# Weights split in plain order with strided views of PSUM, and stationary columns taken 4 and 2 apart, in a two-layer encoder trunk

## Chip, core and metric

The kernel runs on one core of one Trainium2 chip. The metric is the device time of one execution in microseconds; the median of three runs of the kernel before is 1271.1 us (1270.49 to 1271.89).

## What is computed

A trunk of two layers over 256 positions of width 1024. Each layer is a half-step feed-forward part, a mixer and another half-step feed-forward part, each with a norm ahead of it and one behind it. The mixer is dilated window attention in layer 0 and two-way retention in layer 1.

```python
def rms_norm(x, g):
    y = x * lax.rsqrt(jnp.mean(x * x, axis=-1, keepdims=True) + NORM_EPS)
    return y * g

def swiglu(h, w_gate, w_up, w_down):
    return (jax.nn.silu(h @ w_gate) * (h @ w_up)) @ w_down

for i in range(DEPTH):                       # DEPTH = 2, D = 1024, D_FF = 2816
    g = norm_gains[i]
    h = swiglu(rms_norm(x, g[0]), ffn_w_gate[i, 0], ffn_w_up[i, 0], ffn_w_down[i, 0])
    x = x + 0.5 * rms_norm(h, g[1])
    hm = rms_norm(x, g[2])
    m = dilated_attention(hm, ...) if i % 2 == 0 else retention(hm, ...)
    x = x + rms_norm(m, g[3])
    h = swiglu(rms_norm(x, g[4]), ffn_w_gate[i, 1], ffn_w_up[i, 1], ffn_w_down[i, 1])
    x = x + 0.5 * rms_norm(h, g[5])
```

The order of the 2816 inner columns of a feed-forward part is free, as long as the rows of its down matrix come in the same order.

## The kernel before

All weights are read once from memory, 235 MB, in groups of 1 MB into two `raw` buffers (`Stream.dma`). A group has two pieces of 1024 numbers per partition. `Stream.split` makes each piece into a rounded high part (ScalarE, lines 131 and 137) and the rest as low part (VectorE, lines 132 and 138), in a ring of six `w` tiles, and for the first pieces of a part in spare tiles (`wx`). Every product of activations with weights is then three matmuls: high by high, low by high, high by low. With a gain (lines 137 and 138) a piece is split in two instructions of 512, without one (down and output matrices, lines 131 and 132) in one of 1024.

There are two forms of product. In the first (`piece`, `mm3`, lines 217 to 219) the activations are stationary and 512 weight columns move; the down matrices, attention's v, retention's v and gates, and the first two units of each feed-forward part are computed so. In the second (`unit_t`, lines 414 to 416) the weights are stationary, a block of 128 columns at a time, and 256 positions move; units 2 to 10 of each feed-forward part and attention's and retention's q and k are computed so. Pieces for the second form are called `still`. A part has ten units of 512 columns (gate and up in turn, `h` for a pair) and an eleventh of 256 gate and 256 up columns.

The moving operand is always read with `alternate`: one element from the first half of the columns, one from the second. In the first form the split therefore reads `raw` with `deal`, two elements apart, and writes two halves, so that the columns land in PSUM in their own order. In the second form the positions land in PSUM in alternating order, and `tiles` reads them from there two apart.

At the end of a part `down` finishes the first 128 positions (`t` = 0) of the last five rows ahead of the second; `post` takes the square sum of each half on ScalarE (line 295) and the product with the gain on VectorE (line 296), then a few Newton steps, and adds to `x` (line 302). `pre_half` transposes the new `x` on TensorE (line 259) into the next part's `xh` and `xl`. ScalarE and VectorE run their instructions in the order given; the splits of the next part's first weights stand between those of `post`. In the first two units of a part the transposes of the first `h` (`h_store`, line 449) wait for `row_end` (line 432), a row of the norm's scales.

Of the kernel before, what the change touches and what calls it, by code (L numbers as in the profile page):

```python
# [14 lines left out]
P = 128  # L15
# [11 lines left out]
def deal(z):  # L27

    return z.rearrange("p (h c a) -> p h a c", a=2, c=256)


def halves(z):
    return z.rearrange("p (h a c) -> p h a c", a=2, c=256)


def alternate(z):

    return z.rearrange("p (a c) -> p c a", a=2)


class Stream:
# [18 lines left out]
    def add_rows(self, srcs, rows, norm, still=False):  # L60

        first = len(self.pieces)
        for k0 in range(0, rows, 4):
            g = len(self.groups)
            self.groups.append(("rows", srcs, k0))
# [7 lines left out]
    def add_down(self, src, rows):  # L73

        first = len(self.pieces)
        for k0 in range(0, rows, 2):
            g = len(self.groups)
            self.groups.append(("down", src, k0))
            for j in range(2):
                self.pieces.append((g, j, None))  # L80
        return list(range(first, len(self.pieces)))

    def dma(self, halves=False, queue=None):
        if self.n_dma >= len(self.groups):
            return
        kind, src, k0 = self.groups[self.n_dma]
        nc = self.K.nc
        queue = queue or nc.sync
        raw = self.K.sb.tile([P, 2048], F32, tag="raw", bufs=self.raw_bufs, name=f"raw{self.n_dma}")
        if kind == "rows":  # L90
            r = raw.rearrange("p (k c) -> p k c", k=4)
            c = 0
            for ap in src:
                w = ap.shape[1]
                n = 2 if halves else 4
                for i in range(0, 4, n):
                    queue.dma_start(
                        r[:, i : i + n, c : c + w],
                        ap[(k0 + i) * P : (k0 + i + n) * P, :].rearrange("(k p) c -> p k c", p=P),
                    )  # L100
                c += w
        else:
            nc.sync.dma_start(
                raw.rearrange("p (k c) -> p k c", k=2),
                src[k0 * P : (k0 + 2) * P, :].rearrange("(k p) c -> p k c", p=P),
            )
        self.raw[self.n_dma] = raw
        self.n_dma += 1

    def split(self):  # L110
# [16 lines left out]

        view = (lambda z: z) if i in self.still else deal
        flat = (lambda z: z) if i in self.still else halves
        if gain is None:  # L130
            nc.scalar.activation(flat(hi), view(raw), AF.Copy)  # L131
            nc.vector.tensor_tensor(out=flat(lo), in0=view(raw), in1=flat(hi).bitcast(F32), op=ALU.subtract)  # L132
        else:
            for kk in range(2):
                s = slice(kk * 512, kk * 512 + 512)
                gc = self.K.gcol[:, gain + kk : gain + kk + 1]
                nc.scalar.activation(flat(hi[:, s]), view(raw[:, s]), AF.Copy, scale=gc)  # L137
                nc.vector.scalar_tensor_tensor(  # L138
                    out=flat(lo[:, s]), in0=view(raw[:, s]), scalar=gc, in1=flat(hi[:, s]).bitcast(F32),
                    op0=ALU.mult, op1=ALU.subtract,  # L140
                )
# [21 lines left out]
class Trunk:  # L163
# [123 lines left out]
    def post(self, t, banks, gb, name, eps=None):  # L287
# [48 lines left out]

    def plan_ffn(self, l, i):
# [8 lines left out]
        return dict(units=units, down=self.ws.add_down(wd, DFF // P), l=l, n=n)  # L346
# [18 lines left out]
    def ffn_t(self, u, pieces, name, natural, st):  # L365
# [4 lines left out]
        self.unit_t(pieces, accs)  # L370
# [29 lines left out]
    def unit_t(self, pieces, accs, quota=2):  # L400
# [3 lines left out]
        for j, pc in enumerate(pieces):  # L404
            hi, lo = self.ws.get(pc)
            for kk in range(2):
                k = 2 * j + kk
                xh, xl = (alternate(z[:, k, 0 : 2 * P]) for z in (self.xh, self.xl))
                for c in range(4):
                    b, a = divmod(c, 2)  # L410
                    out = accs[b][:, a * 256 : a * 256 + 256]
                    s = slice(kk * 512 + c * P, kk * 512 + c * P + P)

                    mm(out, hi[:, s], xh, start=k == 0 and a == 0, stop=False, skip_group_check=True)  # L414
                    mm(out, hi[:, s], xl, start=False, stop=False, skip_group_check=True)  # L415
                    mm(out, lo[:, s], xh, start=False, stop=k == NK - 1, skip_group_check=True)  # L416
# [26 lines left out]
    def h_store(self, c, t, h, w, natural):  # L443
# [4 lines left out]
        for k in range(nk):  # L448
            nc.tensor.transpose(tr[:, k * P : (k + 1) * P], h[:, k * P : (k + 1) * P], self.ident)
# [25 lines left out]
    def ffn(self, plan, nxt):  # L475
        nc, sb = self.nc, self.sb
        l, n = plan["l"], plan["n"]
        name = f"f{l}{n}"
        natural = l == 0 and n % 6 == 4
        st = {}  # L480
        for u, pieces in enumerate(plan["units"]):
# [17 lines left out]
            if u == 0:  # L499
                sg = []  # L500
                for t in range(2):
                    g = sb.tile([P, 512], F32, tag="sg", bufs=2, name=f"sg_{name}{c}{t}")
                    nc.scalar.activation(g, accs[t], AF.Silu, scale=self.rstd[:, t : t + 1])
                    sg.append(g)
            else:
                self.pend.append(lambda: self.row_end(name))
                for t in range(2):
                    h = sb.tile([P, 512], F32, tag="h", bufs=2, name=f"h_{name}{c}{t}")
                    nc.vector.tensor_tensor(out=h, in0=accs[t], in1=sg[t], op=ALU.mult)
# [139 lines left out]
    def attn(self, plan, nxt):  # L649
# [5 lines left out]
        for u, (o, kind, g, pieces) in enumerate(plan["units"]):  # L655
# [28 lines left out]
            if kind != "v":  # L684
# [14 lines left out]
                for t in range(2 if u == 0 else 0):  # L699
                    nat = sb.tile([P, 512], F32, tag="h", bufs=2, name=f"nat{u}{t}")  # L700
                    nc.scalar.activation(nat, accs[t], AF.Copy, scale=(rq if kind == "q" else self.rstd)[:, t : t + 1])
# [17 lines left out]
            else:  # L719
                if g == 0:  # L720
                    V = sb.tile([P, 6, 512], F32, tag="D", name=f"V{o}")
                    for t in range(2):
                        nc.vector.tensor_scalar(out=V[:, t, :], in0=accs[t], scalar1=self.rstd[:, t : t + 1], scalar2=None, op0=ALU.mult)
                else:

                    for t in range(2):
                        rs = self.rstd if g == 1 else ru
                        for half in range(2):
                            r = 2 * t + half if g == 1 else (2 * t + 1 + half) % 4
                            hs = slice(half * 64, half * 64 + 64)  # L730
                            if half == 0:
                                nc.vector.tensor_scalar(out=V[hs, 2 + r, :], in0=accs[t][hs, :], scalar1=rs[hs, t : t + 1], scalar2=None, op0=ALU.mult)
                            else:
                                nc.scalar.activation(V[hs, 2 + r, :], accs[t][hs, :], AF.Copy, scale=rs[hs, t : t + 1])
# [162 lines left out]
    def ret(self, plan, nxt):  # L897
# [6 lines left out]
        for u, (h, kind, pieces) in enumerate(plan["units"]):  # L904
# [16 lines left out]
            elif kind == "v":  # L921
                vv = sb.tile([P, 2, 2, 512], F32R, tag="C1", name=f"vv{h}")
                st["vh"], st["vl"] = vv[:, 0], vv[:, 1]
                for t in range(2):
                    rs = self.rstd[:, t : t + 1]
                    vh, vl = (halves(st[z][:, t, :]) for z in ("vh", "vl"))
                    nc.scalar.activation(vh, deal(accs[t]), AF.Copy, scale=rs)
                    nc.vector.scalar_tensor_tensor(out=vl, in0=deal(accs[t]), scalar=rs, in1=vh.bitcast(F32), op0=ALU.mult, op1=ALU.subtract)
# [3 lines left out]
            else:  # L932
                d = 0 if kind == "gf" else 1
                sg = []
                for t in range(2):
                    g = sb.tile([P, 512], F32, tag="sg", bufs=2, name=f"rsg{u}{t}")
                    nc.scalar.activation(g, accs[t], AF.Silu, scale=self.rstd[:, t : t + 1])
# [55 lines left out]
    def rt_gate(self, st, d, sg):  # L993
# [9 lines left out]
        for t in range(2):  # L1003
            if d == 0:
                w = st["C2"][:, 512 * t : 512 * t + 512]
                st["w", t] = w
                nc.vector.scalar_tensor_tensor(out=w, in0=st["y", d][t], scalar=mv[:, t, 0:1], in1=sg[t], op0=ALU.subtract, op1=ALU.mult)
                nc.vector.tensor_scalar(out=w, in0=w, scalar1=r[:, t : t + 1], scalar2=None, op0=ALU.mult)
            else:
                nc.vector.scalar_tensor_tensor(out=sg[t], in0=st["y", d][t], scalar=mv[:, t, 0:1], in1=sg[t], op0=ALU.subtract, op1=ALU.mult)  # L1010
# [77 lines left out]
```

## Time and profile before

| | us |
|---|---|
| median of three runs | 1271.1 |
| the profiled execution, own time | 1272.25 |
| its span, first to last instruction | 1270.5 |
| TensorE matmul busy | 1228.0 |
| weight loads busy | 1125.8 |
| VectorE busy | 941.8 |
| ScalarE busy | 789.0 |
| DMA queue of the weights, share of 16 engines | 57% |

Busy time of matmuls counts overlapping ones as one stretch, so the rate of TensorE is read from the starts of neighbouring matmuls. Weight loads overlap matmuls. The chain of waits follows the work back from the last instruction to whatever released it; where it runs through an engine other than TensorE, the time of that engine sets when TensorE may go on.

### The profile page before, as it was taken

Reading aid. Unit: us, or ns where it says so; the run is one execution under the profiler, and the core shown is the slowest. Engines: PE = TensorE matmul, PEld = TensorE weight load, DVE = VectorE, ACT = ScalarE, POOL = GpSimd, SP = SyncE. Lnnn points to the kernel's source line nnn. Section 1 sums busy time; section 2 is a strip of 40 time slices with the busy share of each in tenths; the row PEclk is TensorE's granted clock in tenths of the full one; section 3 lists DMA queues with packets and bytes.
Section 4 is the critical chain, followed back from the end, with each engine's and each line's share of the span. In section 5 each row is a group of like instructions: output and inputs, shape, how many; then the busy total and the mean of one; then the engine's idle time right before and its main releaser. Section 6 shows DMA issues by size and latency. Waiting matters only on the chain.

```text
span 1270.5 us, 21059 instructions
## 1 busy us (share of the span) xinstructions
PE 1228.0 (97%) x8532; PEld 1125.8 (89%) x8532; DVE 941.8 (74%) x1615; ACT 789.0 (62%) x1065; POOL 19.4 (2%) x17
## 2 busy tenths in 40 slices
PE   8999999999999999999989999998999999999997
PEld 7999987977998778999879999887998988899986
DVE  6776668678568868887577766688999987776665
ACT  6656665467456666876666666655766767565662
POOL 1000001000000000000000000000000000000000
PEclk9999999999999999999999999999999999999999
DMA  7756566763764355665646665645565546466552
GB/s 219 235 179 198 192 211 182 228 206 117 216 216 166 122 165 190 194 217 196 202 137 221 195 197 196 204 145 168 168 185 175 166 167 209 142 228 200 192 196 77
DMA packets 130270, 235.75 MB, mean 186 GB/s; under 512 B 25451, under 2 KB 42075, under 8 KB 130172
## 3 DMA queue, kind: packets, MB, share of 16 engines
q1 hardware_dynamic: 129372, 233.04, 57.0%
q8 instruction: 67, 1.10, 0.3%
q10 hardware_dynamic: 800, 1.36, 0.3%
q14 instruction: 31, 0.25, 0.1%
HBM read 232.21 MB, written 1.12 MB: 184 GB/s over the span
## 4 chain that ended last, share of the span: by engine, by line
PE 71%; DVE 15%; DMA 8%; ACT 5%; issue 1%; DVEq 0%; POOL 0%; ACTq 0%; SPq 0%; POOLq 0%
PE ac_f L416 9%; PE ac_f L414 9%; PE ac_f L415 9%; DVE w L138 7%; PE d_f L217 5%; PE d_f L219 5%; PE d_f L218 5%; DMA raw<-in_ffn_w_gate_dram 4%; PE rt L219 3%; PE rt L217 3%; PE rt L218 3%; PE at L414 3%; PE at L416 3%; PE at L415 3%; ACT w L137 1%
## 5 line engine op out<-in xcount | busy, mean ns | idle before, releaser
L137 ACT ACTIVATE w<-raw,gcol 128x512 fp32r<-128x512 f32 x596 | 427.6, 777 | 253.7 <-PE ac_f L416 72.6
L138 DVE SCALAR_TENSOR_TENSOR w<-raw,gcol,w 128x512 fp32r<-128x512 f32 x596 | 437.6, 781 | 134.0 <-ACT w L137 131.9
L132 DVE TENSOR_TENSOR w<-raw,w 128x1024 fp32r<-128x1024 f32 x112 | 166.9, 1492 | 97.2 <-ACT w L131 96.2
L131 ACT ACTIVATE w<-raw 128x1024 fp32r<-128x1024 f32 x112 | 174.4, 1561 | 100.3 <-DMA raw<-in_ffn_w_down_dram 38.6
L217 PE MATMUL d_f<-w,hhf 128*128 128x512 f32 x352 | 134.7, 383 | 0.0
L218 PE MATMUL d_f<-w,hhf 128*128 128x512 f32 x352 | 134.4, 382 | 0.0
L219 PE MATMUL d_f<-w,hlf 128*128 128x512 f32 x352 | 134.2, 381 | 0.0
L414 PE MATMUL at<-xh_f,w 128*128 128x256 f32 x352 | 96.9, 276 | 0.0
L415 PE MATMUL at<-xl_f,w 128*128 128x256 f32 x352 | 96.9, 275 | 0.0
L416 PE MATMUL at<-xh_f,w 128*128 128x256 f32 x352 | 96.8, 275 | 0.0
L414 PE MATMUL ac_f<-xh_in,w 128*128 128x256 f32 x288 | 79.6, 276 | 0.0
L416 PE MATMUL ac_f<-xh_in,w 128*128 128x256 f32 x288 | 79.4, 276 | 0.0
L414 PE MATMUL ac_f<-xh_f,w 128*128 128x256 f32 x288 | 79.3, 275 | 0.0
L415 PE MATMUL ac_f<-xl_at,w 128*128 128x256 f32 x288 | 79.3, 275 | 0.0
L415 PE MATMUL ac_f<-xl_f,w 128*128 128x256 f32 x288 | 79.3, 275 | 0.0
L415 PE MATMUL ac_f<-xl_rt,w 128*128 128x256 f32 x288 | 79.3, 275 | 0.0
L414 PE MATMUL ac_f<-xh_at,w 128*128 128x256 f32 x288 | 79.3, 275 | 0.0
L414 PE MATMUL ac_f<-xh_rt,w 128*128 128x256 f32 x288 | 79.3, 275 | 0.0
L416 PE MATMUL ac_f<-xh_at,w 128*128 128x256 f32 x288 | 79.2, 275 | 0.0
L416 PE MATMUL ac_f<-xh_f,w 128*128 128x256 f32 x288 | 79.2, 275 | 0.0
L415 PE MATMUL ac_f<-xl_in,w 128*128 128x256 f32 x288 | 79.2, 275 | 0.0
L416 PE MATMUL ac_f<-xh_rt,w 128*128 128x256 f32 x288 | 79.2, 275 | 0.0
(350 smaller groups left out, 2971.0 us busy)
## 6 DMA issues: line engine op xcount, KB each, us to landing
raw<-in_ffn_w_down_dram SPq DMA_DIRECT2D x44, 1024.0 KB, 4.8
raw<-in_ffn_w_up_dram SPq DMA_DIRECT2D x40, 1024.0 KB, 5.0
raw<-in_ffn_w_gate_dram SPq DMA_DIRECT2D x39, 1024.0 KB, 5.0
raw<-in_attn_w_in_dram SPq DMA_DIRECT2D x36, 1024.0 KB, 5.1
raw<-in_ret_w_in_dram SPq DMA_DIRECT2D x24, 1024.0 KB, 5.4
raw<-in_ret_w_in_dram SPq DMA_DIRECT2D x16, 512.0 KB, 4.5
raw<-in_ret_w_out_dram SPq DMA_DIRECT2D x8, 1024.0 KB, 4.7
raw<-in_ffn_w_gate_dram SPq DMA_DIRECT2D x8, 512.0 KB, 3.9
```

The costliest lines, as they stand in the source:

```text
L131: nc.scalar.activation(flat(hi), view(raw), AF.Copy)
L132: nc.vector.tensor_tensor(out=flat(lo), in0=view(raw), in1=flat(hi).bitcast(F32), op=ALU.subtract)
L137: nc.scalar.activation(flat(hi[:, s]), view(raw[:, s]), AF.Copy, scale=gc)
L138: nc.vector.scalar_tensor_tensor(out=flat(lo[:, s]), in0=view(raw[:, s]), scalar=gc, in1=flat(hi[:, s]).bitcast(F32), op0=ALU.mult, op1=AL ...
L217: mm(out, xh, wh, start=start, stop=False)
L218: mm(out, xh, wl, start=False, stop=False)
L219: mm(out, xl, wh, start=False, stop=stop)
L414: mm(out, hi[:, s], xh, start=k == 0 and a == 0, stop=False, skip_group_check=True)
L415: mm(out, hi[:, s], xl, start=False, stop=False, skip_group_check=True)
L416: mm(out, lo[:, s], xh, start=False, stop=k == NK - 1, skip_group_check=True)
```

## The change

`Stream.split` no longer deals: every piece is read and written in plain order. The moving weights are still read with `alternate`, so their columns now land in PSUM in alternating order, and whoever reads such a bank does it through `undo`, two elements apart: post-norm, gate, h, attention's first q and k and its V, retention's v, gates and the group-norm products. Square sums and group-norm statistics read a bank as before.

In `unit_t` the 128 stationary columns of a block may lie `step` apart. `STEPS` gives 4 for the first feed-forward part, 2 for the second and 1 for the other two; the eleventh unit takes at most 2. This changes the order of the inner columns, so `h_store` transposes the same columns, and the down matrix is loaded so that a partition takes `step` neighbouring rows, two of them in one load (8 KB in a row). Retention's and attention's blocks keep step 1.

The order of instructions is the same on TensorE, VectorE, ScalarE and GpSimd. On SyncE the loads of the first two down matrices (22) have another form, at the same places.

```diff
-def deal(z):
-
-    return z.rearrange("p (h c a) -> p h a c", a=2, c=256)
+def alternate(z):
+
+    return z.rearrange("p (a c) -> p c a", a=2)
+
+
+def stepped(c, step):
+
+    first = c // step * P * step + c % step
+    return slice(first, first + (P - 1) * step + 1, step)
+
+
+def undo(z):
+
+    return z.rearrange("p (c a) -> p a c", a=2)
 
 
 def halves(z):
-    return z.rearrange("p (h a c) -> p h a c", a=2, c=256)
+    return z.rearrange("p (a c) -> p a c", a=2)
...
-            self.groups.append(("down", src, k0))
+            self.groups.append(("down", src, k0, min(step, 2) if k0 >= 20 else step))
...
-                src[k0 * P : (k0 + 2) * P, :].rearrange("(k p) c -> p k c", p=P),
+                src[k0 * P : (k0 + 2) * P, :].rearrange("(k p) c -> p k c", p=P) if step == 1
+                else src[k0 // step * step * P :][: step * P].rearrange("(p k) c -> p k c", k=step)[:, k0 % step : k0 % step + 2],
...
-        view = (lambda z: z) if i in self.still else deal
-        flat = (lambda z: z) if i in self.still else halves
         if gain is None:
-            nc.scalar.activation(flat(hi), view(raw), AF.Copy)
-            nc.vector.tensor_tensor(out=flat(lo), in0=view(raw), in1=flat(hi).bitcast(F32), op=ALU.subtract)
+            nc.scalar.activation(hi, raw, AF.Copy)
+            nc.vector.tensor_tensor(out=lo, in0=raw, in1=hi.bitcast(F32), op=ALU.subtract)
...
-                nc.scalar.activation(flat(hi[:, s]), view(raw[:, s]), AF.Copy, scale=gc)
+                nc.scalar.activation(hi[:, s], raw[:, s], AF.Copy, scale=gc)
...
-            nc.vector.tensor_tensor(out=yg[:, s], in0=banks[h], in1=gb[:, s], op=ALU.mult)
+            nc.vector.tensor_tensor(out=halves(yg[:, s]), in0=undo(banks[h]), in1=halves(gb[:, s]), op=ALU.mult)
...
+    STEPS = (4, 2, 1, 1)
...
-        self.unit_t(pieces, accs)
+        self.unit_t(pieces, accs, step=self.step if u < 10 else min(self.step, 2))
...
-                    s = slice(kk * 512 + c * P, kk * 512 + c * P + P)
-
-                    mm(out, hi[:, s], xh, start=k == 0 and a == 0, stop=False, skip_group_check=True)
-                    mm(out, hi[:, s], xl, start=False, stop=False, skip_group_check=True)
-                    mm(out, lo[:, s], xh, start=False, stop=k == NK - 1, skip_group_check=True)
+                    s = stepped(c, step)
+                    wh, wl = (z[:, kk * 512 : kk * 512 + 512][:, s] for z in (hi, lo))
+
+                    mm(out, wh, xh, start=k == 0 and a == 0, stop=False, skip_group_check=True)
+                    mm(out, wh, xl, start=False, stop=False, skip_group_check=True)
+                    mm(out, wl, xh, start=False, stop=k == NK - 1, skip_group_check=True)
...
-            nc.tensor.transpose(tr[:, k * P : (k + 1) * P], h[:, k * P : (k + 1) * P], self.ident)
+            nc.tensor.transpose(tr[:, k * P : (k + 1) * P], h[:, stepped(k, self.step)], self.ident)
...
-                    nc.scalar.activation(g, accs[t], AF.Silu, scale=self.rstd[:, t : t + 1])
+                    nc.scalar.activation(halves(g), undo(accs[t]), AF.Silu, scale=self.rstd[:, t : t + 1])
...
-                    nc.scalar.activation(vh, deal(accs[t]), AF.Copy, scale=rs)
+                    nc.scalar.activation(vh, undo(accs[t]), AF.Copy, scale=rs)
```

## Rows read from the trace of the kernel before

**Rows 1.** The page: busy times, and the chain that ended last by engine.
```profile
PE 1228.0 (97%) x8532; PEld 1125.8 (89%) x8532; DVE 941.8 (74%) x1615; ACT 789.0 (62%) x1065; POOL 19.4 (2%) x17
...
PE 71%; DVE 15%; DMA 8%; ACT 5%; issue 1%; DVEq 0%; POOL 0%; ACTq 0%; SPq 0%; POOLq 0%
```
**Rows 2.** Busy by stretch (PE, PEld, DVE, ACT, POOL, clock, DMA, GB/s): gate/up, down.
```profile
90.00:100.00 10.00, 10.00 (x92) 10.00 (x91) 6.29 (x10) 6.38 (x10) 0.00 (x0) 1.00 0.58 190
150.00:160.00 10.00, 10.00 (x48) 8.75 (x47) 5.77 (x4) 6.11 (x5) 0.00 (x0) 1.00 0.62 196
```
**Rows 3.** List in order of time, TensorE, gate/up: start us, us, what.
```profile
99.83 0.28 PE L414 MATMUL ac_f<-xh_in,w 128*128 128x256 f32 x1
...
100.39 0.28 PE L416 MATMUL ac_f<-xh_in,w 128*128 128x256 f32 x1
```
**Rows 4.** The same list, TensorE, down.
```profile
150.66 0.38 PE L217 MATMUL d_f<-w,hhf 128*128 128x512 f32 x1
...
151.52 0.38 PE L218 MATMUL d_f<-w,hhf 128*128 128x512 f32 x1
```
**Rows 5.** The same list, weight loads, just after a wait of TensorE.
```profile
45.52 0.19 PEld L416 LDWEIGHTS ac_f<-xh_in,w 128*128 128x128 f32 x1
...
45.62 0.19 PEld L414 LDWEIGHTS ac_f<-xh_in,w 128*128 128x128 f32 x1
```
**Rows 6.** The chain of waits in order of time, first part to attention: start us, us.
```profile
179.99 1.65 ACT w L131
181.67 1.54 DVE w L132
183.23 5.21 DMA raw<-in_attn_w_in_dram
...
189.45 3.59 DVE wx L138 x4
```
**Rows 7.** The list in order of time, ScalarE, at the same place.
```profile
188.46 3.66 ACT L137 ACTIVATE wx<-raw,gcol 128x512 fp32r<-128x512 f32 x4 [1.16 <-DMA raw<-in_attn_w_in_dram]
192.00 0.60 ACT L295 ACTIVATE psq_f<-d_f 128x512 f32<-128x512 f32 x1
```
**Rows 8.** The list, TensorE, at two changes of part; idle time before in brackets.
```profile
196.33 1.32 PE L259 MATMUL xtr_f<-ident,x 128*128 128x128 f32 x8 [2.12 <-DVE x L302]
...
1080.39 1.29 PE L259 MATMUL xtr_rt<-ident,xn 128*128 128x128 f32 x8 [1.72 <-DVE xn L302]
```
**Rows 9.** Stretches of 4 us at changes of part: TensorE busy, granted clock, DMA.
```profile
196.00:200.00 4.00, 3.67 (x14) 0.69 0.37 145
...
646.00:650.00 4.00, 1.17 (x8) 1.00 0.79 249
```
**Rows 10.** The list, ScalarE and VectorE, splits in plain order.
```profile
192.78 2.56 ACT L137 ACTIVATE w<-raw,gcol 128x512 fp32r<-128x512 f32 x4
...
207.93 2.73 DVE L138 SCALAR_TENSOR_TENSOR w<-raw,gcol,w 128x512 fp32r<-128x512 f32 x4
```
**Rows 11.** The list, VectorE, dealt splits at the start.
```profile
14.44 3.74 DVE L138 SCALAR_TENSOR_TENSOR w<-raw,gcol,w 128x512 fp32r<-128x512 f32 x4 [0.16 <-ACT w L137]
```
**Rows 12.** Who waited for whom: us in total, times, longest.
```profile
PE htr L449 <- DVE row_f L432: 7.0, 4, 2.2
```
**Rows 13.** Evictions: by form (busy, mean ns); ScalarE's by line (ns min/median/max).
```profile
L376 DVE TENSOR_TENSOR sg_f<-ac_f,row_f 128x512 f32<-128x512 f32 x36 | 23.2, 683 | 0.0
...
L296 DVE TENSOR_TENSOR yg_f<-d_f,gpost 128x512 f32<-128x512 f32 x16 | 11.0, 688 | 11.3 <-ACT psq_f L295 11.3
...
L927 ACT ACTIVATE vv<-rt,rstd_f x8: 662/674/719, 877.6 to 1014.9; 128x512 fp32r<-128x512 f32 x8
```
**Rows 14.** DMA issues: count, KB each, median us to landing.
```profile
raw<-in_ffn_w_down_dram SPq DMA_DIRECT2D x44, 1024.0 KB, 4.8
```
**Rows 15.** The list, ScalarE writing h: in the first and the second part.
```profile
63.12 1.23 ACT L392 ACTIVATE hhf<-h_f 128x512 fp32r<-128x512 f32 x2 [0.22 <-DVE h_f L383]
...
540.42 2.57 ACT L392 ACTIVATE hhf<-h_f 128x512 fp32r<-128x512 f32 x2 [0.24 <-DVE h_f L383]
```

More of the change, by code (lines that the diff above doesn't have):

```diff
@@ L64, in add_rows @@
             g = len(self.groups)
-            self.groups.append(("rows", srcs, k0))
+            self.groups.append(("rows", srcs, k0, 1))
             for j in range(2):
@@ L71, in add_rows, with add_down @@
         return list(range(first, len(self.pieces)))
-    def add_down(self, src, rows):
+    def add_down(self, src, rows, step=1):
         first = len(self.pieces)
@@ L85, in dma @@
             return
-        kind, src, k0 = self.groups[self.n_dma]
+        kind, src, k0, step = self.groups[self.n_dma]
         nc = self.K.nc
@@ L136, in split @@
                 gc = self.K.gcol[:, gain + kk : gain + kk + 1]
-                nc.scalar.activation(flat(hi[:, s]), view(raw[:, s]), AF.Copy, scale=gc)
+                nc.scalar.activation(hi[:, s], raw[:, s], AF.Copy, scale=gc)
                 nc.vector.scalar_tensor_tensor(
-                    out=flat(lo[:, s]), in0=view(raw[:, s]), scalar=gc, in1=flat(hi[:, s]).bitcast(F32),
+                    out=lo[:, s], in0=raw[:, s], scalar=gc, in1=hi[:, s].bitcast(F32),
                     op0=ALU.mult, op1=ALU.subtract,
@@ L345, in plan_ffn @@
         units.append(self.ws.add_rows([wg[:, 2560:], wu[:, 2560:]], NK, n, True))
-        return dict(units=units, down=self.ws.add_down(wd, DFF // P), l=l, n=n)
+        step = self.STEPS[2 * l + i]
+        return dict(units=units, down=self.ws.add_down(wd, DFF // P, step), l=l, n=n, step=step)
     def piece(self, j, pc, accs, ts, cols=(0, P)):
@@ L398, in tiles, with unit_t @@
         return z.rearrange("p (a c t) -> p a t c", a=2, t=2)
-    def unit_t(self, pieces, accs, quota=2):
+    def unit_t(self, pieces, accs, quota=2, step=1):
         mm = self.nc.tensor.matmul
@@ L477, in ffn @@
         l, n = plan["l"], plan["n"]
+        self.step = plan["step"]
         name = f"f{l}{n}"
@@ L508, in ffn @@
                     h = sb.tile([P, 512], F32, tag="h", bufs=2, name=f"h_{name}{c}{t}")
-                    nc.vector.tensor_tensor(out=h, in0=accs[t], in1=sg[t], op=ALU.mult)
+                    nc.vector.tensor_tensor(out=halves(h), in0=undo(accs[t]), in1=halves(sg[t]), op=ALU.mult)
                     self.pend.append(lambda c=c, t=t, h=h: self.h_store(c, t, h, 512, natural))
@@ L722, in attn @@
                     for t in range(2):
-                        nc.vector.tensor_scalar(out=V[:, t, :], in0=accs[t], scalar1=self.rstd[:, t : t + 1], scalar2=None, op0=ALU.mult)
+                        nc.vector.tensor_scalar(out=halves(V[:, t, :]), in0=undo(accs[t]), scalar1=self.rstd[:, t : t + 1], scalar2=None, op0=ALU.mult)
                 else:
@@ L731, in attn @@
                             if half == 0:
-                                nc.vector.tensor_scalar(out=V[hs, 2 + r, :], in0=accs[t][hs, :], scalar1=rs[hs, t : t + 1], scalar2=None, op0=ALU.mult)
+                                nc.vector.tensor_scalar(out=halves(V[hs, 2 + r, :]), in0=undo(accs[t][hs, :]), scalar1=rs[hs, t : t + 1], scalar2=None, op0=ALU.mult)
                             else:
-                                nc.scalar.activation(V[hs, 2 + r, :], accs[t][hs, :], AF.Copy, scale=rs[hs, t : t + 1])
+                                nc.scalar.activation(halves(V[hs, 2 + r, :]), undo(accs[t][hs, :]), AF.Copy, scale=rs[hs, t : t + 1])
                 if g == 2:
@@ L936, in ret @@
                     g = sb.tile([P, 512], F32, tag="sg", bufs=2, name=f"rsg{u}{t}")
[L937 removed]
+                    nc.scalar.activation(halves(g), undo(accs[t]), AF.Silu, scale=self.rstd[:, t : t + 1])
                     sg.append(g)
```

10 lines of the change are left out of this document (5 added, 5 removed).

## Prediction

> **What bounds the kernel now.** I read four things in this order: the page's busy times and its chain of work, TensorE's starts in two quiet stretches, the chain and the queues around one change of part, and then the costs of single instructions. The page says that TensorE is busy for 97% of the span and holds 71% of the chain; VectorE holds 15% [rows 1]. In the middle of a gate/up stretch and of a down stretch TensorE is busy for 10.00 of 10 us at full granted clock, while VectorE and ScalarE have some 4 us to spare in each 10 [rows 2]. So there is little to gain inside a stage; what the two split engines save there is slack. How fast TensorE runs is in the start times: five matmuls of 256 columns take 0.56 us from start to start, 112 ns each [rows 3], and four of 512 columns 0.86 us, 215 ns each [rows 4]. In the gate/up form every matmul has its own load of the stationary operand, and two loads that follow each other after a wait start about 0.11 us apart [rows 5]. A load is thus as long as the matmul that covers it; in the down form, at 215 ns a matmul, half of that time is spare. This is the one place where the change can hurt at once.
>
> TensorE's lost time lies where one part ends and the next begins. The chain through the first such place runs over ScalarE's split of a down piece, VectorE's, a DMA, the splits of the next part's first weights, then the post-norm, and only then may TensorE transpose [rows 6]. The queue shows why: ScalarE's square sum of the second half (L295, 192.00) stands behind four weight splits (188.46) [rows 7], and the product with the gain stands behind four on VectorE (189.45) [rows 6]. TensorE waits 2.12 us there and 1.72 at the last such place, the shortest of four that I count after the first three feed-forward parts and retention [rows 8]; the longest leaves it busy for 1.17 of 4 us [rows 9]. [...]
>
> **The change part by part.** The order of instructions on TensorE, VectorE, ScalarE and GpSimd is the same in both kernels; on SyncE too, where the 22 loads of the first two down matrices have another form. So nothing is moved, no wait is added, and only durations change.
>
> *Splits.* Pieces for the moving side were read two elements apart; now they are read and written in a row. Both forms stand side by side: four splits of 512 take 3.66 us on ScalarE and 3.59 on VectorE in the old form [rows 6, 7], 2.56 and 2.73 in the plain one [rows 10], with matmuls of 512 columns beside them. A split of 1024 takes 1.65 and 1.54 us [rows 6]; two plain ones of 512 are 2.56/2 = 1.28 and 2.73/2 = 1.37, an upper bound for one of 1024. Inside stages all of this is hidden under TensorE. At a change of part the chain [rows 6] shortens by 1.65-1.28 = 0.4, 1.54-1.37 = 0.2, the first split by (3.66-2.56)/4 = 0.3, and VectorE's four by 3.59-2.73 = 0.9: together 1.8 us up to the product with the gain. What is late next is the post-norm itself, which TensorE has waited for all along. At four places its wait is about that long or longer, so I take 1.8 each, **7.2 us**. After attention, the fifth, I have a shorter wait and take half, **0.9**. At the start VectorE's four old splits (3.74 us) stand in front of TensorE [rows 11]: 3.74-2.73, **1.0**. The clock's fall costs (1-0.69) x 4 = 1.2 us each time, and there are three such stretches behind changes of part, 3.7 us; if the waits go, these falls may. As the row of 646 us shows that a wait does not decide it alone, I take half, **1.9**, and keep 0 and 3.7.
>
> *Given back.* Some 35 us behind a change of part TensorE waits again, four times, for the first h's transposes: 7.0 us in all, for VectorE's row of scales [rows 12]. On the way there stand plain splits and a DMA that the change leaves as they are. Where TensorE comes earlier and these do not, the new wait eats the gain. I take **2 us** back, between 0 and 7.
>
> *PSUM views.* Evictions now read PSUM two apart: post-norm, gate, h, V and the group norm's product. VectorE has both forms today, 683 ns two apart (L376) and 688 in a row (L296) for 512; ScalarE's 674 two apart (L927) stands against 0.60 us for a square sum in a row [rows 7, 13]. So 0 on VectorE and at most 0.07 us on ScalarE, off the path. Nothing.
>
> *Down loads.* The 22 loads read 8 KB in a row per partition and not two rows of 4 KB. With 4 KB rows they land in 4.8 us [rows 14], a load with 2 KB rows took 5.21 in the chain [rows 6]: twice the row was worth 0.4 us at most, and no wait of TensorE above ends with a down load. Nothing.
>
> *Stationary columns 4 and 2 apart.* A feed-forward part has 9 units in this form, each of 8 x 4 blocks with three loads, 864 loads. In the first part eight units have step 4 (768 loads) and the last step 2 (96); in the second part all 864 have step 2. No row shows a strided load. Two rows stand nearest, on either side. For no cost: the moving operand takes its columns in turn from two places 128 or 256 elements apart, so no two in a row are neighbours, and TensorE still takes one per 0.42 ns (215/512) [rows 4]; a load needs one per 0.86 ns (110/128) [rows 5]. It is the same engine. For a cost: ScalarE's write of h in the second part, whose innermost step is 4, takes 2.57 us for two, and the same instruction in a row 1.23 in the first part [rows 15], 2.1 times. Applied to a load that is 110 to 230 ns, 118 ns more than the 112 on a path without slack: 768 x 0.118 = 91 us. Step 2 has ScalarE's own split as its row, 3.66/2.56 = 1.43: 47 ns, and 960 x 0.047 = 45 us. Below nothing: if the load is what holds the spacing at 112 ns and gets faster, the columns' own rate of 0.42 ns gives 108, and 1728 x 0.004 = 7 us go. I take **0**, since the moving operand is TensorE's own reading and the other rows are another engine's, and keep -7 and +91 (with step 2, +136).
>
> [...]
>
> Sum against the profiled run's own 1272.25 us (span 1270.5): -(7.2+0.9+1.0+1.9)+2 = -9.0, so 1263.25. That run lies 1.15 above the median 1271.1, so I say **1262.1 us**.
>
> **The rivals.**
> 1. *The loads at step 4 are slow.* Place: units 2 to 9 of the first part, where a load has no slack. It decides as soon as a load takes over 112 ns; at 12 ns more it eats the whole gain. By the ScalarE row it costs 91 us: 1353; at the milder 1.43 it is 768 x 0.047 = 36, 1298. Against it: the moving operand's row. [...]
> 2. *Step 2 is slow as well*: 1353+45 = 1398.
> 3. *Nothing can be seen*: later waits and DMAs take the whole gain, 1270 to 1272. For it: TensorE is at 97%, and the chains between parts all pass a DMA; against: the post-norm behind the splits is on the same queues and moves with them.
> 4. *The views cost what the splits saved*: reads of PSUM two apart collide with TensorE as reads of SBUF do. By the splits' difference, (3.66-2.56)/4 = 0.28 us an eviction, two of them ahead of each of five waits cost 2.8: 1265. Against: the rows of VectorE were taken beside matmuls.
>
> **How the numbers follow.** Forecast 0.54 (1252 to 1268: from all of the clock, nothing given back and faster loads, to most of it given back). Evictions that cost more 0.02, still faster. No change to be seen 0.11. Slow loads at step 4 0.28 (1298 to 1353, half of it below 1325), both steps 0.05. To leave no more than 2 in 10 out, the range takes in rival 1: 1252 to 1353; the forecast's own range is 1252 to 1268. Faster by over 0.2% (about what a measurement of this kernel can tell from no change) 0.56, within 0.11, slower 0.33.
>
> **What would show it.** Splits: those of 512 near 0.64 (ScalarE) and 0.68 us, those of 1024 under 1.3 and 1.4, in all stages. Changes of part: the second L295 some 2 us sooner, TensorE's waits for the transposes under 1 us, fewer stretches below full clock. Loads: the start-to-start time of the gate/up matmuls in the first, second and third feed-forward part side by side: 112 ns in all three if I am right, more in the first alone for rival 1, in the first two for rival 2. A longer spacing there would above all make me wrong, for TensorE has no idle time to pay it from.

## The result, and the profile after

The changed kernel takes 1347.22 us (median of four runs, 1346.42 to 1348.89) against 1271.06 for the kernel before: a ratio of 1.0589, 95% interval 1.0572 to 1.0606. It is **slower by 76 us**. The forecast was 1262.1, faster; the time is that of rival 1, loads at step 4 slow, priced there at 1353. The profiled run has a span of 1346.0 us. Lines of `kernel.py` have moved: the splits of 512 are L141 and L142 (before L137 and L138), those of 1024 L135 and L136, the matmuls of the first form L221 to L223 and those of gate/up L423 to L425, the post-norm L299, L300 and L306, the transposes behind it L263.

The page of the kernel after, busy times and the chain by engine; they answer to [rows 1].

```profile
PE 1321.4 (98%) x8532; PEld 1222.6 (91%) x8532; DVE 892.2 (66%) x1615; ACT 695.0 (52%) x1065; POOL 19.7 (1%) x17
...
PE 84%; DVE 8%; DMA 5%; ACT 2%; issue 1%; SPq 0%; DVEq 0%; ACTq 0%
```

ScalarE and VectorE have 94 and 50 us less to do, and TensorE has 93 us more. The list in order of time shows where: TensorE in a gate/up stretch of the first, the second and the third feed-forward part (start us, us, what), as in [rows 3].

```profile
119.62 0.40 PE L423 MATMUL ac_f<-xh_in,w 128*128 128x256 f32 x1
...
121.03 0.40 PE L423 MATMUL ac_f<-xh_in,w 128*128 128x256 f32 x1
...
619.75 0.28 PE L423 MATMUL ac_f<-xh_at,w 128*128 128x256 f32 x1
...
620.71 0.28 PE L425 MATMUL ac_f<-xh_at,w 128*128 128x256 f32 x1
...
799.80 0.28 PE L424 MATMUL ac_f<-xl_f,w 128*128 128x256 f32 x1
...
800.69 0.28 PE L423 MATMUL ac_f<-xh_f,w 128*128 128x256 f32 x1
```

Six matmuls in 1.41 us are 235 ns each at step 4; eight in 0.96 are 120 at step 2 (the median over the whole part is 118); eight in 0.89 are 111 at step 1, as before. In a stretch of the first part, read as in [rows 2], TensorE is never idle and the granted clock is full, so this is no wait:

```profile
100.00:110.00 10.00, 10.00 (x41) 8.65 (x40) 3.41 (x5) 3.71 (x6) 0.00 (x0) 1.00 0.32 107
```

The groups of weight loads by form (busy us, mean ns of one) name the instruction; `xh_in` is the first part, `xh_at` the second, `xh_f` the third:

```profile
L425 PEld LDWEIGHTS ac_f<-xh_in,w 128*128 128x128 f32 x288 | 91.4, 317 | 0.4 <-issue 0.4
...
L425 PEld LDWEIGHTS ac_f<-xh_at,w 128*128 128x128 f32 x288 | 57.0, 198 | 0.0
...
L425 PEld LDWEIGHTS ac_f<-xh_f,w 128*128 128x128 f32 x288 | 55.3, 192 | 0.0
```

The first group mixes 256 loads at step 4 with 32 at step 2. A load's record is longer than the spacing of loads, since they overlap; what counts is the spacing. Just after a wait of TensorE, with no earlier matmul in the way, the list of weight loads shows it as well:

```profile
110.08 0.31 PEld L423 LDWEIGHTS ac_f<-xh_in,w 128*128 128x128 f32 x1 [0.64 <-ACT w L141]
110.29 0.33 PEld L424 LDWEIGHTS ac_f<-xl_in,w 128*128 128x128 f32 x1
```

The second load starts 0.21 us behind the first, where it was about 0.11 before [rows 5].

From the first gate/up matmul to the first down matmul the first part took 129.68 us before and takes 221.99 now. That is **+92.3 us**, or 120 ns for each of 768 loads. All other stages together give 16 us back, the second part's own loss of 4.3 us included, so 76 remain. What they gain is seen at the change from the first part to attention, in the list of ScalarE, VectorE and TensorE (they answer to [rows 7], the last of [rows 6], and the first of [rows 8]), and in stretches of 4 us (busy, granted clock, as in [rows 9]).

```profile
279.35 2.56 ACT L141 ACTIVATE wx<-raw,gcol 128x512 fp32r<-128x512 f32 x4 [0.71 <-DMA raw<-in_attn_w_in_dram]
281.82 0.57 ACT L299 ACTIVATE psq_f<-d_f 128x512 f32<-128x512 f32 x1
...
280.11 2.74 DVE L142 SCALAR_TENSOR_TENSOR wx<-raw,gcol,wx 128x512 fp32r<-128x512 f32 x4 [0.68 <-ACT wx L141]
...
285.95 0.38 PE L223 MATMUL d_f<-w,hlf 128*128 128x512 f32 x1
286.17 1.29 PE L263 MATMUL xtr_f<-ident,x 128*128 128x128 f32 x8
```
```profile
284.60:288.60 4.00, 4.00 (x24) 1.00 0.65 244
...
732.20:736.20 4.00, 3.18 (x18) 1.00 0.66 247
```

The four splits take 2.56 and 2.74 us where they took 3.66 and 3.59. TensorE goes from the down matmul ahead of the transposes (285.95) to the transposes (286.17) with no idle time in brackets, where it waited 2.12 us; the clock stays at 1.00, where it was 0.69. At the longest change it is busy for 3.18 of 4 us, against 1.17.

The other edits in the groups by form and the issues: VectorE's post-norm product and ScalarE's gate of retention, both now reading PSUM two apart, then the same gate before, in a row, and the down loads after (count, KB, median us to landing).

```profile
L300 DVE TENSOR_TENSOR yg_f<-d_f,gpost 128x512 f32<-128x512 f32 x16 | 11.0, 688 | 13.0 <-ACT psq_f L299 13.0
...
L947 ACT ACTIVATE rsg<-rt,rstd_f 128x512 f32<-128x512 f32 x16 | 10.8, 680 | 9.6 <-DVE rstd_f L250 5.0 <-PE rt L223 4.6
```
```profile
L937 ACT ACTIVATE rsg<-rt,rstd_f 128x512 f32<-128x512 f32 x16 | 10.8, 678 | 6.9 <-DVE rstd_f L246 5.0 <-PE rt L219 1.8
```
```profile
raw<-in_ffn_w_down_dram SPq DMA_DIRECT2D x44, 1024.0 KB, 4.8
```

The post-norm product takes 688 ns in either form [rows 13], the gate 680 against 678, and the loads land in 4.8 us as before [rows 14], those in the new form in 5.0 us in the first part and 4.7 in the second: nothing has moved. The other two rows of [rows 13], L376 and L927, were read two apart before as well and test nothing here.

### The profile page after: what moved, and what is told of

It is laid out like the page before. It is cut to its first block, busy times and chain, and to the rows that moved or that the text cites. A ratio compares the mean times of both kernels' runs of the same rounds, so it can differ in the third digit from the quotient of the medians.

```text
span 1346.0 us, 21063 instructions
## 1 busy us (share of the span) xinstructions
PE 1321.4 (98%) x8532; PEld 1222.6 (91%) x8532; DVE 892.2 (66%) x1615; ACT 695.0 (52%) x1065; POOL 19.7 (1%) x17
## 4 chain that ended last, share of the span: by engine, by line
PE 84%; DVE 8%; DMA 5%; ACT 2%; issue 1%; SPq 0%; DVEq 0%; ACTq 0%
PE ac_f L425 12%; PE ac_f L423 12%; PE ac_f L424 12%; PE d_f L221 5%; PE d_f L223 5%; PE d_f L222 5%; DVE w L142 4%; PE rt L221 3%; PE rt L222 3%; PE rt L223 3%; PE at L423 3%; PE at L425 2%; PE at L424 2%; DMA raw<-in_ffn_w_gate_dram 2%; PE at L221 1%; DMA raw<-in_ret_w_in_dram 1%
## 5 line engine op out<-in xcount | busy, mean ns | idle before, releaser
L141 ACT ACTIVATE w<-raw,gcol 128x512 fp32r<-128x512 f32 x596 | 393.3, 714 | 358.3 <-PE ac_f L425 126.9
L142 DVE SCALAR_TENSOR_TENSOR w<-raw,gcol,w 128x512 fp32r<-128x512 f32 x596 | 416.9, 748 | 194.6 <-ACT w L141 191.9
L136 DVE TENSOR_TENSOR w<-raw,w 128x1024 fp32r<-128x1024 f32 x112 | 137.2, 1225 | 123.9 <-ACT w L135 123.7
L135 ACT ACTIVATE w<-raw 128x1024 fp32r<-128x1024 f32 x112 | 118.5, 1058 | 159.1 <-PE d_f L223 91.6
L221 PE MATMUL d_f<-w,hhf 128*128 128x512 f32 x352 | 133.7, 380 | 0.0
L223 PE MATMUL d_f<-w,hlf 128*128 128x512 f32 x352 | 133.4, 379 | 0.0
L425 PE MATMUL ac_f<-xh_in,w 128*128 128x256 f32 x288 | 111.8, 388 | 0.0
L423 PE MATMUL ac_f<-xh_in,w 128*128 128x256 f32 x288 | 111.5, 387 | 0.0
L424 PE MATMUL ac_f<-xl_in,w 128*128 128x256 f32 x288 | 111.3, 386 | 0.0
L423 PE MATMUL at<-xh_f,w 128*128 128x256 f32 x352 | 96.9, 276 | 0.0
L425 PE MATMUL at<-xh_f,w 128*128 128x256 f32 x352 | 96.7, 275 | 0.0
L423 PEld LDWEIGHTS ac_f<-xh_in,w 128*128 128x128 f32 x288 | 91.0, 316 | 1.1 <-ACT w L141 0.6
L425 PEld LDWEIGHTS ac_f<-xh_in,w 128*128 128x128 f32 x288 | 91.4, 317 | 0.4 <-issue 0.4
L424 PEld LDWEIGHTS ac_f<-xl_in,w 128*128 128x128 f32 x288 | 91.2, 317 | 0.0
L423 PE MATMUL ac_f<-xh_at,w 128*128 128x256 f32 x288 | 81.4, 283 | 0.0
L425 PE MATMUL ac_f<-xh_at,w 128*128 128x256 f32 x288 | 81.4, 283 | 0.0
L423 PE MATMUL ac_f<-xh_f,w 128*128 128x256 f32 x288 | 79.3, 275 | 0.0
```

The source lines that it names most:

```text
L135: nc.scalar.activation(hi, raw, AF.Copy)
L136: nc.vector.tensor_tensor(out=lo, in0=raw, in1=hi.bitcast(F32), op=ALU.subtract)
L141: nc.scalar.activation(hi[:, s], raw[:, s], AF.Copy, scale=gc)
L142: nc.vector.scalar_tensor_tensor(out=lo[:, s], in0=raw[:, s], scalar=gc, in1=hi[:, s].bitcast(F32), op0=ALU.mult, op1=ALU.subtract,)
L221: mm(out, xh, wh, start=start, stop=False)
L223: mm(out, xl, wh, start=False, stop=stop)
```

## The experiments

**The views alone, and the steps alone.** Two kernels cut the change in half. The first is the kernel after with

```diff
-    STEPS = (4, 2, 1, 1)
+    STEPS = (1, 1, 1, 1)
```

the second the kernel before with `stepped`, `STEPS = (4, 2, 1, 1)` and the new down loads, its splits dealt as before.

> The change with step 1 everywhere: the views and the plain splits alone. Theory (the trace of the change read by part): the first feed-forward part's units lost 92.3 us and the second's 4.3 us to the strided loads, and all other stretches together gained about 21 us, so the views alone give about 1250 us, with 112 ns between gate/up matmuls in every part. Rival (the prediction's own sum for the views): 9 us of gain, 1262 us. Second rival: the gain seen elsewhere came only because TensorE was slower in the first part and its supply had got ahead; then under 5 us of gain, over 1266 us.

> The kernel before with the stationary steps 4, 2, 1, 1 and the down loads that go with them, but with the old dealt splits and plain reads of PSUM. Theory that both halves add: 1271 + (1347 - 1250) = 1368 us, with 235 ns between gate/up matmuls at step 4 and 118 at step 2. Rival: the slow loads come only together with plain-order splits (their writes meet the loads in another way); then the spacing stays near 112 ns and the time near 1271 us.

The views alone: 1246.83 us, ratio to before 0.9799 (0.9781 to 0.9818). It **beats both kernels**, by about 2% and by 7.5%. The steps alone: 1370.84, ratio 1.0762 (1.0736 to 1.0787). The halves add up, -25.5 and +97 us on 1271 (-2.0% and +7.6%), to within 5 us of the 76 measured. With the splits dealt the gate/up matmuls start 234 ns apart at step 4 and 118 at step 2 (medians of the list), so the slow loads do not come from the plain splits. The loss is all in the steps, and the views with the plain splits hold a gain larger than the one forecast.

**Step 2 everywhere.**

```diff
-    STEPS = (4, 2, 1, 1)
+    STEPS = (2, 2, 2, 2)
```

> The change with step 2 in all four feed-forward parts. Theory: a load at step 2 takes 6 to 7 ns more than the 112 ns that are free, whatever the part; 4 x 864 loads x 6.5 ns = 22 us over the views alone, about 1272 us. Rival: step 2 costs nothing by itself and the 118 ns of the second part come from its strided write of h; then 112 ns in the other three parts and about 1252 us.

Measured 1271.41, ratio 0.9991 (0.9979 to 1.0002): no difference from the kernel before, and 24.6 us more than with step 1. The list shows it in the third part:

```profile
699.74 0.28 PE L423 MATMUL ac_f<-xh_f,w 128*128 128x256 f32 x1
...
700.93 0.28 PE L424 MATMUL ac_f<-xl_f,w 128*128 128x256 f32 x1
```

Ten matmuls in 1.19 us, 119 ns against 112; this part writes h in a row, so the second part's 118 did not come from its strided write of h. Over 4 x 864 loads 7 ns each are 24 us. Step 2 is cheap per load and still eats the whole gain of the views, because such a load takes longer than its matmul every time.

**Steps 1 to 8 side by side.** The views with step 1, but units 2 to 9 of the first part take their stationary columns at steps 1, 3, 4, 5, 6, 7, 8 and 2, for instance

```diff
+                    elif pat == 5:
+                        wh, wl = (z[:, 4 * kk + c : 4 * kk + c + 636 : 5] for z in (hi, lo))
```

> The views with step 1, except that units 2 to 9 of the first feed-forward part take their stationary columns at steps 1, 3, 4, 5, 6, 7, 8 and 2, one step a unit (from step 5 on and at step 3 the columns of a block are other ones than the product wants, so that part of the computation is changed). [...] Rival of growing distance: step 8 clearly slower than 4. Rival of banks met in step with the moving operand: 4 and 8 slow, 5 and 7 near 112 to 118.

One run, 1314.44 us. The median spacing, worked out from the starts in the list, by step: 1: 112; 2: 118; 3: 177; 4: 235; 5: 225; 6: 224; 7: 233; 8: 240 ns. The groups of loads (busy us, mean ns of one) ordered here by step, 1 to 8 (step 1 from the eleventh unit):

```profile
L468 PEld LDWEIGHTS ac_f<-xh_in,w 128*128 128x128 f32 x32 | 6.1, 192 | 0.0
...
L463 PEld LDWEIGHTS ac_f<-xh_in,w 128*128 128x128 f32 x32 | 6.3, 198 | 0.0
...
L433 PEld LDWEIGHTS ac_f<-xh_in,w 128*128 128x128 f32 x32 | 8.5, 265 | 0.0
...
L438 PEld LDWEIGHTS ac_f<-xh_in,w 128*128 128x128 f32 x32 | 10.6, 331 | 0.0
...
L443 PEld LDWEIGHTS ac_f<-xh_in,w 128*128 128x128 f32 x32 | 10.2, 318 | 0.2 <-issue 0.2
...
L448 PEld LDWEIGHTS ac_f<-xh_in,w 128*128 128x128 f32 x32 | 10.2, 319 | 0.0
...
L453 PEld LDWEIGHTS ac_f<-xh_in,w 128*128 128x128 f32 x32 | 10.5, 328 | 0.0
...
L458 PEld LDWEIGHTS ac_f<-xh_in,w 128*128 128x128 f32 x32 | 10.8, 337 | 0.0
```

The price grows by 59 ns a step from 2 to 4 and then stops; 4 columns of 4 bytes are 16 bytes. Counted in pieces of that size, 128 columns at steps 2, 3 and 4 lie on 64, 96 and 128: 118/64, 177/96 and 235/128 are all 1.84 ns. Beyond step 4 every column has its own piece already, and the price stays at 225 to 240. That fits a price per 16 bytes touched from step 2 on, and neither one that grows with the distance nor one for steps 4 and 8 alone (5 and 7 take 225 and 233). For step 1, with 32 pieces, it would give 59 ns; the loads after a wait start about 110 ns apart there [rows 5], so it does not reach down to step 1. Steps 5 and 6 are 10 to 16 ns cheaper than 4 and 8; why, no run shows.

**The moving operand in other orders, and the cover.** In the first part's down, rows 2 to 15 read the moving operand in seven other orders, two rows each; in the second part's down the stationary activations lie 2, 4 and 8 apart under matmuls of 512:

```diff
+            if name == "f00" and 2 <= k < 16:
+                mm3 = (self.mv_plain, self.mv_two, self.mv_four, self.mv_eight, self.mv_streams4, self.mv_streams8, self.mv_streams16)[k // 2 - 1]
+            if name == "f04" and 4 <= k < 16:
+                n = (1, 2, 4)[k // 4 - 1]
+                mm3 = (self.st2, self.st4, self.st8)[k // 4 - 1]
+                o = k % n * 2 + t
+                xh, xl = (z[:, k // n * n : k // n * n + n, :].rearrange("p k c -> p (k c)")[:, o : o + 127 * 2 * n + 1 : 2 * n] for z in (self.hh, self.hl))
```

> The views with step 1 everywhere, and two parts of the computation changed. In the first part's down, rows 2 to 15 give the moving operand other orders, two rows each: in a row, 2 apart, 4 apart, 8 apart, and 4, 8 and 16 places read in turn; the other rows keep two places in turn. In the second part's down the stationary activations are read 2 apart in rows 4 to 7, 4 apart in rows 8 to 11, 8 apart in rows 12 to 15. [...] Stationary under a matmul of 512: 2 apart 215, 4 and 8 apart 235 to 240, the load alone setting the pace. [...] Rival on the cover (moving and stationary reads share one port and add): 4 apart 215+123=338.

One run, 1282.75 us. The groups of matmuls (busy us, mean ns of one), ordered here by pattern. Moving in a row (L230), 2, 4 and 8 apart (L236, L243, L250), 4, 8 and 16 places in turn (L257, L264, L271); then stationary 2, 4 and 8 apart with two moving places in turn (L278, L285, L292):

```profile
L230 PE MATMUL d_f<-w,hlf 128*128 128x512 f32 x8 | 3.1, 389 | 0.0
...
L236 PE MATMUL d_f<-w,hhf 128*128 128x512 f32 x8 | 5.1, 632 | 0.0
...
L243 PE MATMUL d_f<-w,hhf 128*128 128x512 f32 x8 | 5.1, 642 | 0.0
...
L250 PE MATMUL d_f<-w,hhf 128*128 128x512 f32 x8 | 4.9, 610 | 0.0
...
L257 PE MATMUL d_f<-w,hhf 128*128 128x512 f32 x8 | 3.6, 451 | 0.0
...
L264 PE MATMUL d_f<-w,hhf 128*128 128x512 f32 x8 | 5.5, 689 | 0.0
...
L271 PE MATMUL d_f<-w,hhf 128*128 128x512 f32 x8 | 5.0, 627 | 0.0
...
L278 PE MATMUL d_f<-w,hhf 128*128 128x512 f32 x16 | 6.1, 379 | 0.0
...
L285 PE MATMUL d_f<-w,hhf 128*128 128x512 f32 x16 | 6.4, 398 | 0.0
...
L292 PE MATMUL d_f<-w,hhf 128*128 128x512 f32 x16 | 6.5, 403 | 0.0
```

From start to start (medians of the list), a matmul of 512 moving columns takes

| moving order | ns | stationary, under two places in turn | ns |
|---|---|---|---|
| two places in turn | 216 | step 1 | 216 |
| in a row | 227 | step 2 | 216 |
| 2 apart | 451 | step 4 | 236 |
| 4 apart | 461 | step 8 | 240 |
| 8 apart | 432 | | |
| 4, 8, 16 places in turn | 283, 487, 435 | | |

The left half shows that the order counts: two apart doubles the time of a row, 451 ns against 227. Two places in turn is the *cheapest* of the orders tried, better than a row. The loads' price of 1.84 ns per 16 bytes comes near for in a row (128 pieces, 1.77 ns each) and for 2 apart (256, 1.76), but for 4 and 8 apart (512) it would give 942, and 461 and 432 were measured: the moving side stops at 0.84 to 0.90 ns a column. So it is no full account of the moving side, and why 4 in turn lies between, and 8 in turn above 16, stays open.

The right half is as expected for a load that sets the pace alone: under a matmul of 216 ns the step-4 load takes 236 from start to start, near its own 235, and does not add 123. The cover is real, and it is the cover that the gate/up form does not have.

**No order at all.** The views with step 1, the moving operand in a row everywhere, PSUM read in a row; attention's queries and keys are still taken from PSUM in the alternating order, so its positions are permuted there.

```diff
 def alternate(z):
-    return z.rearrange("p (a c) -> p c a", a=2)
+    return z
```

> The views with step 1, and no order in the moving operand at all: 512 and 256 columns in a row, and no views of PSUM. If two places in turn cost the same as a row, 1247 us, within 0.3% of the run with the views alone; evictions unchanged. If the moving order in turn holds a little of TensorE's pace, 215 to 213 ns a matmul, some 6000 matmuls by 1 to 2 ns, 1235 to 1241. If in turn is what keeps the pace (two places read from two banks), slower than 1260.

Measured 1279.04, ratio 1.0047 (1.0032 to 1.0062), 32 us more than with the alternating order. In the first down the list shows five matmuls in 1.14 us, 228 ns each:

```profile
149.89 0.39 PE L223 MATMUL d_f<-w,hlf 128*128 128x512 f32 x1
...
151.03 0.39 PE L222 MATMUL d_f<-w,hhf 128*128 128x512 f32 x1
```

In the gate/up form the spacing goes from 112 to 113 or 114. The third of the expected cases came, at 11 ns a matmul of 512; that two banks are the reason, as it supposed, no run shows.

**The splits alone.** The kernel before, `view` and `flat` in `split` replaced by nothing:

```diff
-        view = (lambda z: z) if i in self.still else deal
-        flat = (lambda z: z) if i in self.still else halves
+        view = flat = lambda z: z
```

> The kernel before with the splits in a row and nothing else: PSUM is read in a row as before, so the columns of what follows stand in another order and that part of the result is changed; times are those of the splits alone. If PSUM read 2 apart costs nothing: 1246 to 1249, as with the views. If it costs 0.28 us an eviction at the changes of part (rival 4 of the prediction): 1242 to 1244.

Measured 1248.88, ratio 0.9818 (0.9799 to 0.9836). With the views it was 0.9799, so reading PSUM two apart costs nothing that can be told: rival 4, which needed 2.8 us less here than with the views, falls. What that rival said of SBUF shows in the lists before and after. ScalarE's first split of 512, with TensorE idle, takes 0.75 us two apart and 0.71 in a row; beside the down's matmuls they take 0.96 to 1.03 and 0.70 to 0.72 each (L137 at 188.46 before, L141 at 279.35 after). With VectorE idle, a split of 1024 beside gate/up matmuls takes 1.41 us two apart and 1.06 in a row, so it is not VectorE's splits alone that make the one two apart slow:

```profile
7.87 0.75 ACT L137 ACTIVATE w<-raw,gcol 128x512 fp32r<-128x512 f32 x1
...
133.25 1.41 ACT L131 ACTIVATE w<-raw 128x1024 fp32r<-128x1024 f32 x1 [1.29 <-PE ac_f L416]
```
```profile
7.72 0.71 ACT L141 ACTIVATE w<-raw,gcol 128x512 fp32r<-128x512 f32 x1
...
225.04 1.06 ACT L135 ACTIVATE w<-raw 128x1024 fp32r<-128x1024 f32 x1 [1.79 <-PE ac_f L425]
```

**Where the splits pay.** The same splits in a row near a change of part only, and inside the stages only.

```diff
+        view, flat = (deal, dealt) if i in self.old else (lambda z: z, lambda z: z)
```

> The views with step 1, but only pieces near a change of part are split in a row: the last 6 rows of a down matrix, the first two units of a feed-forward part, the first of retention, and all query and key units of attention as before. The other down rows, attention's value units and retention's value and gate units keep the old order in their splits, so their columns are permuted (that part of the result is changed). If splits inside a stage are hidden, as the prediction took it: 1247 to 1249. If the 16 us that the prediction missed come from inside the stages (attention's softmax, retention's row statistics, later waits): 1256 to 1264.

> The other half of the run with plain splits at the changes of part: here the pieces near a change keep the old order in their splits, and the first down rows, attention's value units and retention's value and gate units are split in a row (the columns of the pieces in the old order are permuted, that part of the result is changed). At the changes alone gave 18 us of the 24 to 26 of all. If the two places add: 6 to 8 us less than before, 1265 to 1267. If what is saved inside a stage only counts once TensorE comes earlier into it: 1270 to 1272. If the splits inside a stage overlap with those at its end, so that either alone does most of it: 1258 to 1262.

Near the changes: 1254.55, ratio 0.9855 (0.9839 to 0.9872), 18 us. Inside: 1265.25, ratio 0.9942 (0.9926 to 0.9959), 7.5 us. Together 25.6, the gain of the whole: the places add. The first run's time lies between its two expected ranges, 1.5 us under the second, so part of the gain does come from inside the stages. The waits of TensorE (us in total, times, longest), first near the changes, then inside:

```profile
PE htr L471 <- DVE row_f L454: 3.9, 3, 2.0
...
PE xtr_f L276 <- DVE xn L319: 2.2, 3, 1.2
```
```profile
PE htr L471 <- DVE row_f L454: 7.8, 4, 2.8
PE xtr_f L276 <- DVE xn L319: 4.6, 2, 2.4
```

The lines are L449, L432, L259 and L302 of the kernel before; there they were 7.0 [rows 12] and 5.0. Plain splits near the changes cut both; those inside leave both.

What is won inside is mostly in the two mixers: with the splits inside alone, attention's units take 234.2 us against 237.7, retention's 199.5 against 201.4. TensorE around the softmax, first the kernel before, then the views with step 1:

```profile
286.20 1.52 PE L810 MATMUL ptt<-ident,pr 128*128 128x128 f32 x6 [2.90 <-DVE pr L803]
...
288.36 0.63 PE L219 MATMUL at<-w,xl_f 128*128 128x512 f32 x1
288.79 0.63 PE L217 MATMUL at<-w,xh_f 128*128 128x512 f32 x1
```
```profile
281.04 0.88 PE L820 MATMUL ptt<-ident,pr 128*128 128x128 f32 x6 [1.61 <-DVE pr L813]
...
282.19 0.38 PE L223 MATMUL at<-w,xl_f 128*128 128x512 f32 x1
282.40 0.38 PE L221 MATMUL at<-w,xh_f 128*128 128x512 f32 x1
```

The wait for VectorE's product is 1.61 us and not 2.90, and after it the matmuls start 0.21 us apart and not 0.43: the granted clock did not fall. With either half of the splits alone it still falls at this place (0.72 in 6 us), after a wait of 2.9 us in the one and 1.8 in the other. Why it holds only with both stays open.

## Why the prediction was wrong

**The step that failed is "Stationary columns 4 and 2 apart", taken as 0.** The prediction bounded the load from two sides, by the moving operand [rows 4] and by ScalarE's step-4 write [rows 15], and chose the first because it is TensorE's own reading. Measured at step 4 are 235 ns a load in place of 112, and 92.3 us. The moving operand's row showed one special order. "No two in a row are neighbours" was read as "every column costs a fetch of its own". Two places read in turn come back to a column's neighbour with every second column, and the run with other orders shows that it is the best case tried: 216 ns, against 451 two apart. That the coming back is the reason is an inference; the times are what was measured. The row was a bound for nothing but itself.

**The other end came out right.** ScalarE's factor of 2.1 gave 118 ns more a load and 91 us; measured are 120 and 92.3. Why a write on ScalarE and a load on TensorE share the factor, no run says. Step 2 costs 118 to 120 ns in place of 112: near nothing for one load, 24.6 us over four parts. For the moving operand step 2 is not cheap, 451 against 227. In the second part the units took 127.83 us against 123.50 before and 121.97 with the views alone, so step 2 cost 4 to 6 us there, where rival 2 had 45.

**The bound said what it needed to.** "A load is as long as the matmul that covers it" held at step 1, and what is over costs in full: with 112 ns of cover step 4 costs 123 ns, with 216 it costs 20. Rival 1 named the place, the price and the point at which it decides, and the spacing in three parts side by side told it from the others, as the prediction asked. What was wrong is the choice between the two ends. That rival 1's 1353 lies within 6 us of the measured time is partly luck: the steps cost 97 us and not 91, and the rest gained 25.5 and not 9; the two misses offset.

**Splits.** Of 512 they took 0.64 and 0.69 us at the change of part, and of 1024, over the whole kernel, 1.06 and 1.23, under the bounds of 1.3 and 1.4 (before 1.49 on VectorE). Their worth on the path was put at 9 us and is 25.5 in the run with the views alone. Term by term (us; the first three from the times between the stages' first matmuls in the list, before and in the run with plain splits near the changes; the fourth is the other run's median):

| term | as predicted | measured |
|---|---|---|
| changes of part, each with the down stage ahead of it and the clock | -10.0 | -11.4 (-3.4, -0.7, -1.6, -3.0, -2.7) |
| start, with the first part's units | -1.0 | -0.1 |
| given back behind a change, all later units | +2 | -5.3 |
| splits inside the stages | 0 | -7.5 |

The first term was nearly right, and by its parts: TensorE's idle time at the five changes (the brackets of the list) fell from 9.8 us to 2.1, which is 7.7 where I said 8.1. The other 3.8 fit the clock's falls (0.69, 0.67 and 0.69 in the 4 us from 196, 831 and 1080 us before), 3.7 by the 0.69 of [rows 9] if all of them go, where I took half; no stretch around these changes is below 1.00 there. The start gave its 1.0 and lost it again. The first two units took 25.6 us from first to last matmul before and 24.6 here. But behind TensorE's wait for the first h's transposes the granted clock now fell, as a stretch of 10 us shows (length, TensorE busy, granted clock, DMA), first before, then with plain splits near the changes:

```profile
40.00:50.00 10.00, 7.94 (x70) 1.00 0.77 241
```
```profile
40.00:50.00 10.00, 8.02 (x58) 0.83 0.75 241
```

So the first part's units took 129.68 us before and 129.61 here, 129.71 with the views alone, where the clock fell as well. Why it fell here and not before stays open: the wait is as long (2.0 us against 2.1). The third has the **wrong sign**: I had held the splits ahead of the row of scales for those that the change leaves as they are. But the first two units are of the moving form and their pieces were dealt; with the pieces near a change in a row, these among them, the row of scales came earlier still and the wait of 7.0 us shrank to 3.9, 3.1 of the 5.3; with them dealt and the others in a row it stayed at 7.8. The fourth, "inside stages all of this is hidden under TensorE", holds for gate/up and down stretches. It fails where TensorE waits for VectorE inside a stage, as in attention's softmax and in retention's row statistics (4.7 us before, 3.2 and 3.3 with either half of the splits).

**PSUM views and down loads**: nothing, as said; the views by the rows of the profile after and by the splits alone, the loads by their 4.8 us.

## What to carry to other kernels

A strided operand that a row shows to be free is free in that order alone; before it stands for another, count the pieces of 16 bytes that the other touches, and measure it: here the loads went by them (118, 177 and 235 ns for 64, 96 and 128), the moving operand only up to 256 (227 and 451 ns for 128 and 256, then 461 and 432 for 512). Weights that are used once and loaded for 256 columns leave no slack under a matmul, so even 7 ns a load cost 25 us over 3456 of them; the same step 4 under 512 columns would have cost a sixth as much per load. And where an engine off the bound gets faster, look for its queue at every place where the bound engine waits for it, not only at the stage boundaries.

## What the runs showed of the hardware

- A weight load of 128 columns of 4 bytes took 118, 177 and 235 ns at steps 2, 3 and 4, which is 1.84 ns per 16 bytes touched, then 225 to 240 up to step 8.
- Of the orders tried, the moving operand of 512 columns is fastest when read from two places in turn (216 ns), slower in a row (227), and half as fast 2, 4 or 8 apart (432 to 461). Left in a row throughout, the kernel takes 32 us more.
- A slow load and a fast moving operand overlap in full: 236 ns under a matmul of 216, for a load that sets a pace of 235 under one of 112.
- PSUM read two apart by VectorE and ScalarE costs nothing (688 and 680 ns against 688 and 678 in a row), while SBUF read two apart next to matmuls cost 1.3 to 1.4 times (four splits 3.66 against 2.56 us on ScalarE, 3.59 against 2.74 on VectorE).
